# Cached keys of an encoder step copied in SBUF to an fp32r tile and transposed from it, for head pair 0 also transposed as fp32

## The chip, the cores and the metric

The kernel runs on one core of one Trainium2 chip. The metric is the device time of one execution in microseconds (us). The engines are named as in the profile: PE is TensorE (matmuls and transposes; PEld are its weight loads), DVE is VectorE, ACT is ScalarE, POOL is GpSimd, SP is SyncE, which here only issues DMAs. Each engine takes its own instructions in the order in which the kernel gives them. SBUF is the memory beside the engines (128 partitions), PSUM the one into which TensorE writes.

## The reference

One layer of a streaming encoder. 1024 new prompt frames and 64 frames of a running stream go through one input projection to 6144 columns; two attention branches with 8 heads of 64 follow, "sb" (stick breaking) and "cb" (a softmax over a band with a bias); their outputs are gated, projected, merged, projected again and added to the input. The change touches the keys of the running stream: its queries attend to 512 cached keys and the 64 new ones.

```python
# x_sample (1, 64, 1024); cache_sb_k, cache_cb_k (1, 1, 512, 8, 64)
sq2, sk2, sv2, sz2, cq2, ck2, cv2, cz2, gs2, gc2 = project(y_s, norm_w[l], w_in[l], q_norm_w[l], k_norm_w[l])
k_all = jnp.concatenate([cache_sb_k[l].astype(sk2.dtype), sk2], axis=1)
o_sb2 = stick_breaking(sq2, k_all, v_all, s_qpos, sb_s_kpos)
kb = jnp.concatenate([cache_cb_k[l].astype(ck2.dtype), ck2], axis=1)
o_cb2 = band_attention(cq2, kb, vb, s_qpos, cb_s_kpos, rel_bias[l])
```

Both attentions need the scores q.k, so the cached keys are needed with the head dimension in the partitions, that is transposed.

## The kernel before

All data is fp32. A matmul is made from operands of the type fp32r. A value that has to keep its precision is split: a high part, written as fp32r by ScalarE, and a low part, the difference, by VectorE or GpSimd. A product is then three matmuls (high by high, low by high, high by low).

The kernel's order is written out by hand; nothing is reordered by a scheduler. It has these stages, by the lines of their matmuls in the trace: a first projection whose result has the frames in the partitions (L464, 10.8 to 227.6 us), a second one with the columns in the partitions (L634, 227.7 to 405.5), attention with the rest of the projection filled in between (L773, L1024, L1115, 405.6 to 856.9), the projections of the two branches (L873, L917, to 926.0) and the last one (L1407, to 1013.6).

The change lies in the first stage. Its loop runs over `i`, eight groups of 256 columns (`NB`), and within it over `ti`, nine tiles of frames in the order `TO` = 8, 0, 1, ..., 7, where tile 8 holds the 64 frames of the running stream. One tile (i, ti) is:

- 24 matmuls (16 for tile 8) into a PSUM tile "acc" (L464); there are three such tiles, two in `psF` and one in `psA`, which serves every third tile;
- `post_nat` (L339), where one is due: two transposes of an older tile of queries or keys into the PSUM tile "pk" (L349), ScalarE's high part (L353), VectorE's low part (L354), and DMAs of whole blocks to DRAM;
- `evac_nat` (L296): for value columns (groups 0 and 5 for "sb", 6 and 7 for "cb") ScalarE copies to "vst", which has three buffers (L305), and SyncE stores it twice (L307, L309); for queries and keys of "cb" ScalarE copies and squares (L319, L320), VectorE sums (L321), GpSimd takes the power -1/2 (L248, L249). For tile 8 a fold of two halves comes before (`fold`, L292 and L293);
- `norm_nat` (L325) of the tile before: two multiplications by VectorE (L329, L330), and for keys a store (L334, L336);
- at set tiles, the splitting of the next group's weights (L115, L122) with the load of those after them (L109), and the steps on the cached keys.

The cached keys go through two steps. `cache_load` (L362) at (0, 4) for "sb" and at (2, 3) for "cb" loads the 512 x 512 keys of a branch into the SBUF tile "ck" (1 MB, one buffer; L365). `cache_pair` (L368) takes one pair of heads, that is 128 of the 512 columns, at (1, 1), (1, 4), (1, 7) and (2, 1) for "sb" and two groups later for "cb": four transposes into the PSUM tile "pc", which has one buffer in `psK` (L371), ScalarE's high part (L373), VectorE's low part (L374), and a store to DRAM (`rdma`, L51) from "hc". Attention loads that back much later. The tile "ck" is used once more, at (4, 2), for the bias table (L238).

`rdma` (L49) is a DMA on SyncE's queue with both sides taken as fp32. A transpose is a matmul whose weights are the tile to transpose, with the identity matrix `ident` streamed through.

Of the kernel before, what the change touches and what calls it, by code (L numbers as in the profile page):

```python
# [8 lines left out]
F32 = mybir.dt.float32  # L9
F32R = mybir.dt.float32r  # L10
AF = mybir.ActivationFunctionType
OP = mybir.AluOpType
# [20 lines left out]
def hybrid_step_kernel(ctx: ExitStack, tc: tile.TileContext, x_prompt, x_sample, c_sbk, c_sbv, c_cbk, c_cbv,  # L33
# [3 lines left out]
    V, A, G, TE, SP = nc.vector, nc.scalar, nc.gpsimd, nc.tensor, nc.sync  # L37
# [11 lines left out]
    def rdma(out, in_):  # L49
        out, in_ = (a if isinstance(a, bass.AP) else a[:] for a in (out, in_))  # L50
        SP.dma_start(out.bitcast(F32), in_.bitcast(F32))  # L51
# [42 lines left out]
    ident = consts.tile([128, 128], F32, name="ident")  # L94
# [103 lines left out]
    with ExitStack() as ph:  # L198
        sx = ExitStack()
        natx = sx.enter_context(tc.tile_pool(name="natx", bufs=2))  # L200
        pn = ph.enter_context(tc.tile_pool(name="pn", bufs=2, side="right"))
        p1x = ExitStack()
        p1 = p1x.enter_context(tc.tile_pool(name="p1", bufs=2))
        psA = ph.enter_context(tc.tile_pool(name="p1acc", bufs=1, space=PS))
        psT = ph.enter_context(tc.tile_pool(name="p1tr", bufs=2, space=PS))
        psK = ph.enter_context(tc.tile_pool(name="p1k", bufs=1, space=PS))
# [3 lines left out]
        xts, xns, hl, cks = {}, {}, {}, {}  # L210
# [19 lines left out]
        half = pn.tile([128, 8], F32, name="half", bufs=1)  # L230
        G.memset(half, -0.5)
        wqk = pn.tile([128, 2, 64], F32, name="wqk", bufs=1)

        rbs = {}

# [126 lines left out]
        def cache_load(b):  # L362
            src = c_sbk if b == "sb" else c_cbk
            ck = p1.tile([128, 4, 512], F32, name="ck", bufs=1)
            SP.dma_start(ck, src.rearrange("(t p) c -> p t c", p=128))  # L365
            cks[b] = ck

        def cache_pair(b, p):  # L368
            pt = psK.tile([128, 4, 128], F32, name="pc")
            for t in range(4):  # L370
                TE.transpose(pt[:, t], cks[b][:, t, p * 128:(p + 1) * 128], ident)  # L371
            h = p1.tile([128, 2, 512], F32R, name="hc", bufs=1)
            A.activation(h[:, 0], pt[:].rearrange("p t c -> p (t c)"), AF.Copy)  # L373
            V.tensor_tensor(out=h[:, 1], in0=pt[:].rearrange("p t c -> p (t c)"), in1=h[:, 0].bitcast(F32),  # L374
                            op=OP.subtract)
            rdma(d_cT[b][p], h)

        raws, blk, sums = {}, {}, {}
# [71 lines left out]
        for i in range(nb):  # L450
            for ti, t in enumerate(TO):
# [38 lines left out]
                if ti in (3, 6) and i > 0 or ti in (5, 6) and i == 0:  # L490
                    h = 1 if ti == 6 else 0
# [30 lines left out]
                if (i, ti) in ((0, 4), (2, 3)):  # L522
                    cache_load("sb" if i == 0 else "cb")
                at = {(1, 1): 0, (1, 4): 1, (1, 7): 2, (2, 1): 3}
                if (i, ti) in at:
                    cache_pair("sb", at[i, ti])
                if (i - 2, ti) in at:
                    cache_pair("cb", at[i - 2, ti])
                if (i, ti) in ((1, 1), (1, 5)):
                    for s in range(2):  # L530
                        h = ti // 4
# [637 lines left out]
    for i in range(len(seq) + LAG + 1):  # L1169
        m = 0  # L1170
        if i < len(seq):
            b, p, t, hd = seq[i]
# [22 lines left out]
        if 0 <= i - LAG < len(seq):  # L1195
            tr(i - LAG)
            b, p, t, hd = seq[i - LAG]
# [182 lines left out]
    for i in range(2):  # L1380
# [3 lines left out]
        for q, s in enumerate(OP_):  # L1384
# [14 lines left out]
            for c in range(2) if s != "b" else ():  # L1399
# [9 lines left out]
                p = ps[:]  # L1409
# [15 lines left out]
                if s in (3, 4, 5, 6):  # L1425
# [4 lines left out]
                    if s == 4:  # L1430
                        p, x = u3[c], xrs.pop((i, 1, 1, c))
# [61 lines left out]
```

## Time and profile before

| | us |
|---|---|
| three runs | 1012.43, 1017.04, 1018.64 |
| median | 1017.04 |
| profiled execution, its time | 1019.66 |
| profiled execution, its span (first to last instruction) | 1017.8 |
| first stage (L464), first to last matmul start | 10.8 to 227.6 |
| transposes of the cached keys (L371), 32 in all | 50.5 to 132.7 |

The mean granted TensorE clock of the profiled execution is 0.993 of full speed. In the rows of the profile that follow, a timeline row gives the start in us, the duration in us, engine, line, operation, output and inputs, and in brackets the idle time of that engine just before, with what ended it. A row of a stretch gives its length and the busy time of PE, PEld, DVE, ACT and POOL with their instruction counts, then the granted clock, the mean busy share of the DMA engines, and GB/s. A row of a group gives the count, the busy time in us and the mean ns of one. A row of DMA issues gives their number, the size of each and the median us from issue to landing.

### The profile page before, as it was taken

What the parts mean: (1) busy time and instruction counts of PE and PEld (TensorE: products, weight loads), DVE (VectorE), ACT (ScalarE), POOL (GpSimd) and SP (SyncE); (2) the same over time, 40 slices, a digit from 0 to 9 for tenths busy, and PEclk for the clock granted to TensorE, in tenths of its full rate; (3) what the DMA queues carried; (4) which work ended last, traced back from release to release, by engine and by line L of the source; (5) the groups of instructions that cost most, each with busy time, mean ns of one, the idle gap of its engine ahead of it and who ended that gap; (6) DMA issues with size and microseconds to landing.
All of it is one profiled execution on the core that took longest, in us unless ns stands there. A gap on an engine that the chain in (4) does not pass through costs nothing. (4 is left out here: it accounts for less than half of the span.)

```text
span 1017.8 us, 20166 instructions
## 1 busy us (share of the span) xinstructions
PE 983.5 (97%) x7512; PEld 935.4 (92%) x7512; DVE 658.2 (65%) x1233; ACT 474.2 (47%) x1075; POOL 323.9 (32%) x338
## 2 busy tenths in 40 slices
PE   6999999998999999999999999999999999899998
PEld 5999999998999999988888889898988898799998
DVE  5466663894455454199888877566766675588645
ACT  5544442343343433276667656444445443355220
POOL 3376663205354543211111101110103102375452
PEclk9999999999999999999999999999999999999999
DMA  7636467435556332786656554665667854852632
GB/s 239 213 114 206 174 244 278 126 94 155 178 159 178 102 96 84 198 213 181 163 153 164 144 146 126 175 205 150 175 159 213 248 174 148 257 159 70 192 124 97
DMA packets 180866, 169.83 MB, mean 167 GB/s; under 512 B 34913, under 2 KB 167137, under 8 KB 180641
## 3 DMA queue, kind: packets, MB, share of 16 engines
q1 hardware_dynamic: 172048, 160.23, 53.4%
q10 hardware_dynamic: 8720, 8.33, 2.6%
q8 instruction: 59, 0.97, 0.4%
q14 instruction: 39, 0.31, 0.1%
HBM read 109.78 MB, written 58.72 MB: 166 GB/s over the span
## 5 line engine op out<-in xcount | busy, mean ns | idle before, releaser
L122 POOL TENSOR_TENSOR wlo<-wraw,whi 128x1024 fp32r<-128x1024 f32 x30 | 73.8, 2459 | 247.5 <-ACT whi L115 227.0
L773 PE MATMUL acc<-xm,whi 128*128 128x384 f32 (+1 forms) x384 | 128.6, 335 | 0.0
L1044 DVE TENSOR_TENSOR_SCAN kp<-kp,imp 64x576 f32<-64x576 f32 (+8 forms) x72 | 102.7, 1427 | 21.4 <-ACT kp L1027 21.2
L1034 ACT ACTIVATE be<-be,sm 128x640 f32<-128x640 f32 (+5 forms) x72 | 50.8, 705 | 97.5 <-DVE sm L1030 97.5
L1076 PE MATMUL pt<-ident,be 128*128 128x128 f32 (+2 forms) x608 | 89.7, 271 | 6.3 <-DVE wT L1087 3.4
L1085 ACT ACTIVATE wT<-pt 128x512 f32<-128x512 f32 (+3 forms) x130 | 63.5, 502 | 54.9 <-PE pt L1076 54.7
L1076 PEld LDWEIGHTS pt<-ident,be 128*128 128x128 f32 (+2 forms) x608 | 68.2, 140 | 18.3 <-issue 6.4
L464 PE MATMUL acc<-whi,xa 128*128 128x256 f32 x256 | 74.2, 292 | 0.0
L773 PEld LDWEIGHTS acc<-xm,whi 128*128 128x128 f32 x384 | 72.5, 189 | 1.1
L464 PE MATMUL acc<-whi,xm 128*128 128x256 f32 x256 | 70.8, 278 | 0.0
L464 PE MATMUL acc<-wlox,xm 128*128 128x256 f32 x256 | 70.8, 278 | 0.0
L464 PE MATMUL acc<-wlo,xa 128*128 128x256 f32 x256 | 70.7, 278 | 0.0
L464 PE MATMUL acc<-whix,xb 128*128 128x256 f32 x256 | 70.7, 278 | 0.0
L464 PE MATMUL acc<-whix,xm 128*128 128x256 f32 x256 | 70.6, 278 | 0.0
L1115 PE MATMUL o<-wT,vp 128*64 128x256 f32 (+1 forms) x608 | 66.6, 360 | 0.0
L1045 DVE TENSOR_TENSOR be<-be,kp 64x576 f32<-64x576 f32 (+8 forms) x72 | 60.3, 837 | 9.6
L1027 ACT ACTIVATE kp<-z 128x384 f32<-128x384 f32 (+6 forms) x112 | 54.2, 484 | 24.4 <-PE z L1025 22.9
L773 PE MATMUL acc<-xa,wlo 128*128 128x384 f32 (+1 forms) x192 | 65.4, 341 | 0.0
L773 PE MATMUL acc<-xa,whi 128*128 128x384 f32 (+1 forms) x192 | 65.3, 340 | 0.0
L773 PE MATMUL acc<-xm,wlo 128*128 128x384 f32 (+1 forms) x192 | 65.1, 339 | 0.0
L1115 PEld LDWEIGHTS o<-wT,vp 128*64 128x64 f32 x608 | 42.7, 138 | 23.4 <-issue 8.0
L773 PE MATMUL acc<-xb,whi 128*128 128x384 f32 (+1 forms) x192 | 64.0, 334 | 0.0
(298 smaller groups left out, 3028.1 us busy)
## 6 DMA issues: line engine op xcount, KB each, us to landing
wraw<-in_w_in_dram SPq DMA_DIRECT2D x35, 512.0 KB, 4.5
wrawx<-in_w_in_dram SPq DMA_DIRECT2D x13, 512.0 KB, 4.3
sq<-d_qsbT SPq DMA_DIRECT2D x32, 192.0 KB, 4.4
sq<-d_qcbT SPq DMA_DIRECT2D x32, 192.0 KB, 4.0
gt<-d_gsb SPq DMA_DIRECT2D x30, 192.0 KB, 3.3
xt<-in_x_prompt_dram SPq DMA_DIRECT2D x8, 512.0 KB, 5.2
d_kcbT<-hl SPq DMA_DIRECT2D x8, 512.0 KB, 4.4
d_qcbT<-hl SPq DMA_DIRECT2D x8, 512.0 KB, 5.6
```

What stands on the lines that cost most here:

```text
L122: (eng or G).tensor_tensor(out=l, in0=raw, in1=h[:].bitcast(F32), op=OP.subtract)
L464: TE.matmul(ps, x, w, start=m == 0, stop=m == len(steps) - 1)
L773: TE.matmul(ps[:, :b - a], w[:, k], xk(x, k)[:, a:b], start=k == 0 and n == 0, stop=k == KT - 1 and n == 2)
L1027: A.activation(kp[:r, x:y], z[:r, :m], AF.Sigmoid, scale=-0.125)
L1034: A.activation(be[:r, :n], be[:r, :n], AF.Exp, bias=kp[:r, j:j + 1], scale=-1.0, accum_out=kp[:r, 2:3])
L1044: V.tensor_tensor_scan(kp[:r, n - 1::-1], kp[:r, n - 1::-1], im[:, ::-1], 0.0, op0=OP.mult, op1=OP.add)
L1045: V.tensor_tensor(out=be[:r, :n], in0=be[:r, :n], in1=kp[:r, 1:n + 1], op=OP.mult)
L1076: TE.transpose(pt[:kr, x, :r], be[:r, kb * 128:kb * 128 + kr], ident[:r, :r])
L1085: A.activation(w[:, sl:sl + m, q0:q0 + r], pt[:, :m, :r], AF.Copy)
L1115: TE.matmul(o[hd * 64:hd * 64 + 64, c0:c1], vv[:kr, kb, hd * 64:hd * 64 + 64], wT[b, p, j, hd, s // 4][:kr, s % 4, c0:c1], start=si == 0, ...
```

## The change

A second identity, `identr`, is made as fp32r. `cache_load` copies "ck" within SBUF, by a DMA, to a tile "cr" of type fp32r, and `cache_pair` transposes from that. For pair 0 of either branch the transposed tile is copied out of PSUM, the same keys are transposed from "ck" as fp32 into another tile of the name "pc", the difference of both is taken, multiplied by 8192 and added to the fp32 one, and this sum is split into high and low part.

```diff
         wqk = pn.tile([128, 2, 64], F32, name="wqk", bufs=1)
+        identr = pn.tile([128, 128], F32R, name="identr", bufs=1)
+        V.tensor_copy(identr, ident)
...
             SP.dma_start(ck, src.rearrange("(t p) c -> p t c", p=128))
-            cks[b] = ck
+            cr = p1.tile([128, 4, 512], F32R, name="cr", bufs=1)
+            rdma(cr, ck)
+            cks[b] = ck, cr
 
         def cache_pair(b, p):
-            pt = psK.tile([128, 4, 128], F32, name="pc")
+            pt = psK.tile([128, 4, 128], F32R, name="pc")
             for t in range(4):
-                TE.transpose(pt[:, t], cks[b][:, t, p * 128:(p + 1) * 128], ident)
+                TE.transpose(pt[:, t], cks[b][1][:, t, p * 128:(p + 1) * 128], identr)
+            src = pt[:].bitcast(F32).rearrange("p t c -> p (t c)")
+            if p == 0:
+
+                d = p1.tile([128, 512], F32, name="cd", bufs=1)
+                V.tensor_copy(d, src)
+                p2 = psK.tile([128, 4, 128], F32, name="pc")
+                for t in range(4):
+                    TE.transpose(p2[:, t], cks[b][0][:, t, p * 128:(p + 1) * 128], ident)
+                s2 = p2[:].rearrange("p t c -> p (t c)")
+                V.tensor_tensor(out=d, in0=s2, in1=d, op=OP.subtract)
+                V.scalar_tensor_tensor(d, d, 8192.0, s2, op0=OP.mult, op1=OP.add)
+                src = d[:]
             h = p1.tile([128, 2, 512], F32R, name="hc", bufs=1)
-            A.activation(h[:, 0], pt[:].rearrange("p t c -> p (t c)"), AF.Copy)
-            V.tensor_tensor(out=h[:, 1], in0=pt[:].rearrange("p t c -> p (t c)"), in1=h[:, 0].bitcast(F32),
-                            op=OP.subtract)
+            A.activation(h[:, 0], src, AF.Copy)
+            V.tensor_tensor(out=h[:, 1], in0=src, in1=h[:, 0].bitcast(F32), op=OP.subtract)
             rdma(d_cT[b][p], h)
```

## The prediction

> **What bounds the kernel now.** I read the busy shares first, then busy time by stretch, then the timelines of TensorE, VectorE, ScalarE and SyncE around the two places where the cached keys are loaded and transposed.
>
> ```profile
> span 1017.8 us, 20166 instructions
> ...
> PE 983.5 (97%) x7512; PEld 935.4 (92%) x7512; DVE 658.2 (65%) x1233; ACT 474.2 (47%) x1075; POOL 323.9 (32%) x338
> ```
>
> ```profile
> 50.00:60.00 10.00, 10.00 (x86) 9.80 (x85) 4.12 (x10) 3.55 (x9) 7.05 (x13) 1.00 0.36 114
> ...
> 104.00:112.00 8.00, 8.00 (x71) 8.00 (x71) 5.08 (x13) 2.98 (x10) 4.45 (x6) 1.00 0.51 182
> ```
>
> TensorE is busy for 97% of the span, and in the two stretches that hold pair 0 of "sb" and of "cb" it is never idle (10.00 of 10.00 us, 8.00 of 8.00). So whatever TensorE waits there is added to the end, and work on other engines or on the DMAs costs only what it makes TensorE wait. These are the instructions around pair 0 of either branch, on TensorE:
>
> ```profile
> 50.36 0.28 PE L464 MATMUL acc<-wlox,xm 128*128 128x256 f32 x1
> ...
> 50.48 0.60 PE L371 MATMUL pc<-ident,ck 128*128 128x128 f32 x4
> ...
> 50.84 0.36 PE L464 MATMUL acc<-whi,xa 128*128 128x256 f32 x1
> ...
> 51.04 0.28 PE L464 MATMUL acc<-whi,xm 128*128 128x256 f32 x1
> ...
> 104.75 0.60 PE L371 MATMUL pc<-ident,ck 128*128 128x128 f32 x4
> ...
> 105.10 0.36 PE L464 MATMUL acc<-whi,xa 128*128 128x256 f32 x1
> ```
>
> and on VectorE, with the nearest row for a copy of 128x512 out of PSUM behind them:
>
> ```profile
> 51.71 0.41 DVE L329 TENSOR_TENSOR qn<-qn,rsn 64x256 f32<-64x256 f32 x1
> ...
> 52.15 0.42 DVE L330 TENSOR_TENSOR qn<-qn,wqk 64x256 f32<-64x256 f32 x1
> 52.50 0.68 DVE L374 TENSOR_TENSOR hc<-pc,hc 128x512 fp32r<-128x512 f32 x1
> ...
> 106.69 0.42 DVE L330 TENSOR_TENSOR qn<-qn,wqk 64x256 f32<-64x256 f32 x1
> 107.04 0.68 DVE L374 TENSOR_TENSOR hc<-pc,hc 128x512 fp32r<-128x512 f32 x1
> ...
> L1087 DVE COPY wT<-pt 128x512 f32<-128x512 f32 x10 | 6.8, 683 | 1.7 <-PE pt L1076 1.7
> ```
>
> The reader is to see the distance between the two engines. TensorE has its four transposes away and is on the next tile at 50.84 and 105.10, while VectorE reaches its work on the same PSUM tile only at 52.50 and 107.04, since the normalisation of the tile before (L329, L330) stands ahead of it. Today nobody waits for that.
>
> **Pair 0: a new wait of TensorE, the main term.** The PSUM tile "pc" has one buffer. The new code transposes into it as fp32r, copies it out with VectorE, and transposes the same keys again, as fp32, into the same buffer. These second transposes wait for the copy, and all matmuls of the next tile are queued behind them on TensorE. The copy takes the place of L374 in VectorE's order: 52.50 + 0.68 = 53.18. From one engine's end to the next one's start I take 0.04 us, by the rows of the fold (47.85 + 0.38 to 48.27):
>
> ```profile
> 46.02 0.39 ACT L305 ACTIVATE vst<-acc 128x256 f32<-128x256 f32 x1 [2.44 <-PE acc L464]
> 47.85 0.38 ACT L292 ACTIVATE fl<-acc 64x256 f32<-64x256 f32 x1 [1.45 <-PE acc L464]
> ...
> 48.27 0.42 DVE L293 TENSOR_TENSOR fl<-acc,fl 64x256 f32<-64x256 f32 x1 [6.47 <-ACT fl L292]
> ...
> 50.25 1.01 POOL L249 TENSOR_TENSOR rsn<-rsn,half 64x4 f32<-64x4 f32 x1
> ```
>
> A group of four fp32 transposes costs 51.04 - 50.48 - 0.12 (the step from 50.36 to 50.48 is that of one matmul) = 0.44 us. So the next tile begins at 53.18 + 0.04 + 0.44 = 53.66 instead of 50.84: +2.8 us. For "cb": 107.04 + 0.68 + 0.04 + 0.44 = 108.20 instead of 105.10: +3.1 us. TensorE is idle 2.4 and 2.6 us of these.
>
> What follows on the pair (subtract 0.68, the scaled add 0.75 by L266's row below, ScalarE's copy, the low part) holds ScalarE's queue until about 3.1 us after the second transposes begin: 0.44 + 0.68 + 0.75 + 0.6 and VectorE's 0.68. ScalarE's next work is the eviction of the tile that TensorE has then just begun, 24 matmuls of 0.12 or 2.8 us behind the transposes' 0.44. It is free again before, so I cost this at nothing; the low part ends beside it. The copy of the identity at the start is one small VectorE instruction before VectorE's first input arrives: nothing.
>
> ```profile
> L266 DVE SCALAR_TENSOR_TENSOR xn<-xt,rs,nw 128x512 f32<-128x512 f32 x16 | 11.3, 747 | 5.7 <-POOL rs L249 5.6
> ...
> 579.45 0.22 PE L1024 MATMUL z<-ks,sq 128*128 128x128 f32 x1
> 579.51 0.28 PE L1025 MATMUL z<-ks,sq 128*128 128x128 f32 x1
> ```
>
> **The transposes in fp32r.** Pair 0's own are before the wait and cost nothing more. The other 24 (three pairs, two branches) go from fp32 at 0.11 to fp32r. No fp32r transpose is in the trace. Two fp32r matmuls of 128 columns stand 0.06 us apart (579.45, 579.51), one of 256 columns takes 0.12. So 24 transposes gain at most 24 x 0.05 = 1.2 us and lose at most 24 x 0.01 = 0.2. Between the row of the same operation and the row of the same type and size I take the middle: -0.6 us.
>
> **The copy in SBUF: two more DMAs of 1 MB, and a held queue.** The copy is issued by SyncE, in order, and waits there until "ck" has landed.
>
> ```profile
> 35.81 0.46 SPq L365 DMA_DIRECT2D ck<-in_cache_sb_k_dram  x1
> 37.64 0.32 SPq L307 DMA_DIRECT2D d_sbv<-vst  x1
> 38.01 0.64 SPq L309 DMA_DIRECT2D out_dram<-vst  x1
> ...
> 87.52 1.26 SPq L365 DMA_DIRECT2D ck<-in_cache_cb_k_dram  x1
> ...
> 95.99 0.36 SPq L336 DMA_DIRECT2D out_dram<-qn  x1
> ...
> ck<-in_cache_sb_k_dram SPq DMA_DIRECT2D x1, 1024.0 KB, 6.2
> ...
> ck<-in_cache_cb_k_dram SPq DMA_DIRECT2D x1, 1024.0 KB, 8.1
> ```
>
> For "sb", SyncE stands from 36.3 to 35.81 + 6.2 = 42.0. Then the copy goes out; no SBUF-to-SBUF transfer is in the trace, so by its own size in "ck"'s row it takes 6.2 (at the least some 5 us, at the most the 8.1 of the other load) and lands at 48.2. TensorE asks for it at 50.5, and even 1.6 us later would do, as VectorE is the last to come: the landing itself costs nothing. But the two stores of "vst" that stood at 37.64 and 38.01 now go out at 42.5 to 43.5, behind 1 MB, and land at about 48.9. "vst" has three buffers, so the eviction of the third tile after, at 46.02, waits for them: 48.9 instead. The fold behind it on ScalarE moves from 47.85 to 49.3, so by 1.4 us, and with it its chain (fold, squares, the power on GpSimd that ends at 51.26, L329). That chain had 0.45 us to spare (51.71 against 51.26), so L329, L330 and the copy move by 1.0 us, and TensorE's wait with them: +1.0 us. With a copy of 5 us it is 0, with one of 8.1 it is about 2.9. The weights whose load is held behind the stores are split two tiles and more later than they land.
>
> For "cb", SyncE had nothing to issue until 95.99, and "ck" lands at 95.6: the hold is nothing. The copy lands at 101.9 to 103.8, ahead of 104.75: nothing, with the landing before TensorE's request as cover.
>
> **The clock.** Idle time of this length has cost clock in this trace. Below are TensorE's three waits with one gap each, and the granted clock by microsecond (seventh figure).
>
> ```profile
> 253.52 0.44 PE L595 MATMUL acc<-ident,s 128*128 128x128 f32 x2 [3.00 <-ACT ko L601]
> ...
> 582.18 1.37 PE L1076 MATMUL pt<-ident,be 128*128 128x128 f32 x8 [2.40 <-DVE wT L1087]
> ...
> 946.69 2.66 PE L1407 MATMUL b<-wo,tk 128*128 128x256 f32 x16 [2.18 <-DVE fl L1449]
> ...
> 255.00:256.00 1.00, 1.00 (x11) 1.00 (x10) 0.51 (x2) 0.99 (x3) 0.00 (x0) 1.00 0.73 243
> ...
> 582.00:583.00 1.00, 0.82 (x7) 0.82 (x8) 1.00 (x2) 0.13 (x1) 0.00 (x0) 0.93 0.16 50
> ...
> 586.00:587.00 1.00, 1.00 (x12) 0.60 (x10) 0.00 (x0) 0.00 (x0) 0.00 (x0) 0.87 0.00 0
> ...
> 948.00:949.00 1.00, 1.00 (x8) 1.00 (x7) 0.22 (x1) 0.00 (x0) 0.00 (x0) 0.54 0.38 72
> ```
>
> Read as a clock of 1.00 or 0.50, these rows put the falls at 582.86 and 948.08 and the rise at 586.26. The stretch of 3.4 us fits a fixed grid, since 948.08 - 582.86 is 107 steps of 3.413 us. The gap of 2.40 us lies whole in the step that ends at 582.86, and the gap of 2.18 has 2.0 us in the step that ends at 948.08: both fell. The gap of 3.00 us is cut by the grid into 1.25 and 1.75 us, and the clock stayed. So a step with about 1.9 us of idle time or more halves the next 3.4 us of work, a price of 1.7 us less what of the gap runs on into it. How the grid lies against the start of another execution the trace can't tell. With the grid anywhere, a gap of 2.6 us ("cb") has 1.9 us in one step in (0.8 + 2 x 0.7) of 3.4 cases, 64%; the gap of "sb", 2.4 + 1.0 = 3.4 us, in 87%, with part of it running on. I take both as falling, at 1.3 and 1.6 us: +2.9 us.
>
> The Trainium skill, "TensorE: Matmul & The Clock Gate", under "Why this matters for your kernels", asks only for "No PE-idle gaps >~3µs between matmul bursts"; its Part 1 has a free-running window of 3413 ns. The window agrees with the grid above, the limit does not: 2.40 and 2.18 us sufficed here. By its limit the clock would stay, and the sum would lose the 2.9 us; that is the second rival.
>
> **The sum.** 2.8 + 3.1 (waits) + 1.0 (held queue) - 0.6 (transposes) + 2.9 (clock) = +9.2 us. The profiled execution took 1019.66 us, 1.86 more than its span, so it would become 1028.9. It is 2.6 above the median of the three runs, 1017.04; against that median I get **1026.2 us**.
>
> **The rivals.**
> Slower by over 1%: the copy in SBUF is slow. SBUF is read and written at once, which no row shows. From a landing at about 49.1 (7.1 us) the held stores cost 0.9 us more, which carries the sum over 1%; at 8.1 us it is 2.9 instead of 1.0: +11.1, 1028.1 us. For it speaks "ck" of "cb" at 8.1, against it that the queue is empty before the copy, having been held.
> The clock stays, or falls once: with one fall the sum is +7.8, with none +6.3, 1023.3 us. For it speaks the gap of 3.00 us that kept its clock, against it the two shorter ones.
> Not slower: the change doesn't do what it says to TensorE, since the second transposes get PSUM of their own beside the first and need not wait. Then there remain two groups of transposes, 0.9 us, less 0.6, and 1017.3 us. Against it: the tile has the same name and one buffer, and the kernel elsewhere takes "xm" anew under one name with another type.
>
> **How the numbers follow.** Forecast 0.45, slow copy 0.25, fewer clock falls 0.24, no wait 0.06. The low bound takes no held stores, the full gain of 1.2 and no fall: 2.8 + 3.1 - 1.2 = +4.7, 1021.7, less some spread of the runs shown (they differ by up to 6 us): 1020. The high bound takes 2.9 for the stores, no gain, both falls at 1.7: +12.2, 1029.2, and the same spread: 1032. The case without a wait and some of the tails stay out. A measurement of this kernel can tell about 1% from no change, 10.2 us here. Over it lie 0.4 of the forecast, three quarters of the slow copy and little of the rest, 0.39 together; faster is left 0.02, within 1% 0.59.
>
> **What would show it.** The timeline of TensorE should have a gap of 2.4 to 3.5 us before the second four transposes at about 51 and one of 2.6 at about 105 to 108, each ended by VectorE's copy; the next tile's matmuls straight after. SyncE should stand at the copy until about 42; ScalarE's eviction at 46.02 should move to about 49. The granted clock should fall to 0.5 for 3.4 us behind either gap. The forecast is wrong if the second transposes start before VectorE's copy ends, if the copy lands after 52, if TensorE waits at other places for evictions or for weights, or if later waits of TensorE shrink by what is lost here.

## The result, and the profile after

| | us |
|---|---|
| before, median of 18 runs (lowest to highest) | 1012.69 (1009.54 to 1018.74) |
| changed, median of 18 runs | 1019.85 (1016.25 to 1023.55) |
| ratio, 95% interval | 1.0058, 1.0041 to 1.0075 |
| profiled execution of the changed kernel, its time and its span | 1018.51, 1016.7 |

The changed kernel is slower by 0.58%, or 5.9 us (4.2 to 7.6) of the 1012.7 before; the two medians by themselves lie 7.2 us apart. The forecast was +9.2 us and 1026.2 us, its range began at 1020.0. The sign was right, the time lies 0.15 us under the range. Of the three runs of before from which the prediction had to start, two lie high among the 18 (1017.04 and 1018.64). Two of the twelve executions of one kernel further down, the changed kernel with its two waits filled, took 1248.78 and 1207.45 us at a granted clock of 0.730 and 0.755, and its median is that of the other ten.

TensorE's timeline of the changed kernel shows the new waits:

```profile
49.84 0.28 PE L479 MATMUL acc<-wlox,xm 128*128 128x256 f32 x1
49.96 0.45 PE L375 MATMUL pc<-identr,cr 128*128 128x128 f32 x4
52.83 0.66 PE L383 MATMUL pc<-ident,ck 128*128 128x128 f32 x4 [2.41 <-DVE cd L380]
53.24 0.36 PE L479 MATMUL acc<-whi,xa 128*128 128x256 f32 x1
53.44 0.28 PE L479 MATMUL acc<-whi,xm 128*128 128x256 f32 x1
...
106.87 0.53 PE L375 MATMUL pc<-identr,cr 128*128 128x128 f32 x4
109.97 0.43 PE L383 MATMUL pc<-ident,ck 128*128 128x128 f32 x1 [2.56 <-DVE cd L380]
```

and VectorE's the instructions that end them:

```profile
51.75 0.42 DVE L332 TENSOR_TENSOR qn<-qn,wqk 64x256 f32<-64x256 f32 x1
52.10 0.68 DVE L380 COPY cd<-pc 128x512 f32<-128x512 f32 x1
53.52 0.69 DVE L385 TENSOR_TENSOR cd<-pc,cd 128x512 f32<-128x512 f32 x1 [0.75 <-PE pc L383]
...
109.24 0.67 DVE L380 COPY cd<-pc 128x512 f32<-128x512 f32 x1
```

TensorE stands idle before the second transposes for 2.41 and 2.56 us, until the copy of the first is out of PSUM, and the copy begins behind L332, where L374 began before. In TensorE's list of waits over the whole span (engine, line, what it waited for: us in total, times, longest) this is the one new group:

```profile
PE pc L383 <- DVE cd L380: 5.0, 2, 2.6
```

5.0 us of waits and 2 x 0.44 us of transposes make 5.9. This execution is nevertheless 1.1 us shorter in its span than the profiled one of before (1016.7 to 1017.8). The reason is elsewhere: that one had waited 3.1 + 1.6 us for weights at 885 us (L917), with a fall of the clock of 6.8 us behind it, and this one 1.1 us. One execution each says nothing about a change of 6 us here; the medians do.

On SyncE and ScalarE the held queue is seen (the last row is one of DMA issues, with the median us to landing):

```profile
35.29 0.46 SPq L367 DMA_DIRECT2D ck<-in_cache_sb_k_dram  x1
41.92 0.50 SPq L51 DMA_DIRECT2D cr<-ck  x1
42.52 0.53 SPq L309 DMA_DIRECT2D d_sbv<-vst  x1
43.11 1.12 SPq L311 DMA_DIRECT2D out_dram<-vst  x1
...
47.46 0.39 ACT L307 ACTIVATE vst<-acc 128x256 f32<-128x256 f32 x1 [4.40 <-DMA out_dram<-vst]
47.87 0.38 ACT L294 ACTIVATE fl<-acc 64x256 f32<-64x256 f32 x1
...
cr<-ck SPq DMA_DIRECT2D x2, 1024.0 KB, 4.9
```

SyncE stands until 41.92, the stores go out behind the copy, and ScalarE waits for them 4.40 us. It is done at 47.85, and the fold begins at 47.87. This execution is 0.5 us ahead of the other there (35.29 against 35.81 for the load), so the fold is 0.5 us late, as much as the chain behind it had to spare: VectorE's copy at 52.10 is 0.1 us later than 52.50 - 0.52. The hold is there and costs next to nothing.

The granted clock (seventh figure) behind the two waits:

```profile
53.00:54.00 1.00, 1.00 (x10) 1.00 (x10) 0.48 (x1) 0.00 (x0) 1.00 (x5) 1.00 0.43 105
...
110.00:111.00 1.00, 1.00 (x5) 1.00 (x6) 0.00 (x0) 0.00 (x0) 0.19 (x1) 0.53 0.00 0
...
113.00:114.00 1.00, 1.00 (x8) 1.00 (x8) 0.69 (x1) 0.15 (x1) 0.00 (x0) 0.77 0.00 0
```

It fell behind the second, from 110.06 to 113.46, and not behind the first.

### The profile page after: what moved, and what is told of

The parts are those of the page before. It is cut to its first block, busy times and chain, and to the rows that moved or that the text cites. A ratio compares the mean times of both kernels' runs of the same rounds, so it can differ in the third digit from the quotient of the medians.

```text
span 1016.7 us, 20197 instructions
## 1 busy us (share of the span) xinstructions
PE 982.3 (97%) x7520; PEld 933.3 (92%) x7520; DVE 660.4 (65%) x1240; ACT 474.5 (47%) x1075; POOL 323.2 (32%) x338
```

## The experiments

The kernels of one set ran on one chip beside the kernel before; the ratios are to that.

### The changed kernel again, as the yardstick

> The changed kernel once more, as the yardstick of the runs beside it. Theory W (TensorE waits for the copy of pair 0 in the one PSUM tile, 2.4 and 2.6 us, pays 0.44 us for each of the two added groups of transposes, and now and then loses 1.7 us to a fall of the clock after a wait): 5.9 us and up to some 2 us more than before. Rival D (the copy in SBUF and its held queue carry a part) and rival T (the fp32r transposes give something back) expect the same of this run.

Measured: 1019.82 us against 1014.63, ratio 1.0057 (1.0037 to 1.0076). The same as in the first set.

### A PSUM tile of its own for the second transposes

```diff
-                p2 = psK.tile([128, 4, 128], F32, name="pc")
+                p2 = psK.tile([128, 4, 128], F32, name="pc2")
```

> The fp32 transposes of pair 0 go to a PSUM tile of their own, so TensorE need not wait for VectorE's copy. W: both gaps vanish, what is left is 0.9 us for the two added groups of transposes, so 0 to 2 us above before and 5 to 7 us under the changed kernel. D: the gaps vanish, but 2 us or more stay. T: at or under before.

Measured: 1014.20 us, ratio 0.9983 (0.9968 to 0.9998). The timeline of TensorE, and of VectorE below it:

```profile
50.17 0.46 PE L375 MATMUL pc<-identr,cr 128*128 128x128 f32 x4
50.47 0.62 PE L383 MATMUL pc<-ident,ck 128*128 128x128 f32 x4
50.85 0.36 PE L479 MATMUL acc<-whi,xa 128*128 128x256 f32 x1
...
52.22 0.68 DVE L380 COPY cd<-pc 128x512 f32<-128x512 f32 x1
```

The eight transposes go through back to back and the next tile starts at 50.85, while VectorE comes to its copy at 52.22, as late as ever. All of VectorE's added work is still there, and the whole loss is gone. So the loss is TensorE's wait for the one PSUM tile. By W 0.9 us should have stayed; the interval ends at 0.2 us under before. About 0.4 us of this the fp32r transposes of the other pairs give back, as the next experiment shows; the rest is not explained.

### The copy in SBUF and the fp32r transposes alone

```diff
-            if p == 0:
+            if p < 0:
```

> The copy in SBUF and the fp32r transposes of all pairs stay, the second transposes of pair 0 with their copy, difference, product and sum are left out. W: within 1 us of before, though ScalarE's eviction is held to about 47.5 us for the stores behind the copy. D: 2 us or more above before. T: 0.5 to 1 us under before, beyond what can be told from this run alone; the timeline then has four fp32r transposes in less than the 0.44 us of the fp32 ones.

Measured: 1011.66 us, ratio 0.9979 (0.9959 to 0.9999). ScalarE's timeline shows the same hold as in the changed kernel:

```profile
47.18 0.39 ACT L307 ACTIVATE vst<-acc 128x256 f32<-128x256 f32 x1 [3.78 <-DMA out_dram<-vst]
47.59 0.38 ACT L294 ACTIVATE fl<-acc 64x256 f32<-64x256 f32 x1
```

Two more DMAs of 1 MB and a queue that stands 6 us cost nothing that shows; rival D falls. That it came out 2 us under before is more than any of the three expected, and is taken up below.

For the fp32r transposes the timeline of a later pair decides. Pair 3 of "sb", in the kernel before and in the changed one, with two transposes of another tile (`pk`) in front of it:

```profile
77.50 0.38 PE L349 MATMUL pk<-ident,qn 128*128 128x128 f32 x2
77.72 0.60 PE L371 MATMUL pc<-ident,ck 128*128 128x128 f32 x4
...
78.27 0.28 PE L464 MATMUL acc<-whi,xm 128*128 128x256 f32 x1
```

```profile
79.86 0.38 PE L351 MATMUL pk<-ident,qn 128*128 128x128 f32 x2
79.99 0.53 PE L375 MATMUL pc<-identr,cr 128*128 128x128 f32 x4
...
80.55 0.28 PE L479 MATMUL acc<-whi,xm 128*128 128x256 f32 x1
```

From the start of the two transposes in front to the same matmul behind the four, it is 78.27 - 77.50 = 0.77 us before and 80.55 - 79.86 = 0.69 us after. The time has to be taken from the same instruction in front: the fp32r group itself starts earlier behind it (0.13 us against 0.22), so from its own start it seems to take as long as the fp32 one, 0.44 us. By this measure every group gains 0.06 to 0.08 us, which makes some 0.4 us for the six groups of pairs 1 to 3. So rival T is right that the fp32r transposes give something back, but it is too little to be told from the times.

### Pair 0 twice as fp32, without the copy

```diff
-            cr = p1.tile([128, 4, 512], F32R, name="cr", bufs=1)
-            rdma(cr, ck)
-            cks[b] = ck, cr
+            cks[b] = ck, ck
...
-            pt = psK.tile([128, 4, 128], F32R, name="pc")
+            pt = psK.tile([128, 4, 128], F32, name="pc")
...
-                TE.transpose(pt[:, t], cks[b][1][:, t, p * 128:(p + 1) * 128], identr)
+                TE.transpose(pt[:, t], cks[b][1][:, t, p * 128:(p + 1) * 128], ident)
```

> No copy in SBUF and no fp32r: the keys of pair 0 are transposed twice as fp32 from the loaded tile, with the copy, difference, product and sum. W: as the changed kernel, 5 to 8 us above before, with the same two gaps of TensorE. D: clearly less than the changed kernel, by 2 us or more. T: above the changed kernel by up to 1 us.

Measured: 1021.72 us, ratio 1.0057 (1.0032 to 1.0081). TensorE has the two waits without the copy too, a little shorter:

```profile
52.71 0.66 PE L381 MATMUL pc<-ident,ck 128*128 128x128 f32 x4 [2.14 <-DVE cd L378]
...
111.57 1.12 PE L381 MATMUL pc<-ident,ck 128*128 128x128 f32 x4 [2.42 <-DVE cd L378]
```

This part alone carries the change.

### All pairs, and the waits filled with matmuls

What is open is the clock. Treating all pairs like pair 0 makes eight waits of two:

```diff
-            if p == 0:
+            if True:
```

> All four pairs of both branches are treated as pair 0 is, so six more waits of TensorE. By the changed kernel's trace VectorE would begin the copy for these at 65.0, 74.9, 82.5, 122.9, 132.5 and 140.0 us, which makes idle times of about 2.6 to 3.6 us, 18.6 together, and 0.44 us for each added group of transposes, 2.6. Theory C (a wait of this length also makes the clock fall behind it in most cases, at up to 1.7 us): 21 us for the waits and transposes and some 5 to 9 us for the clock above the changed kernel, 26 to 30 us in all. Rival N (the clock plays no part that can be seen): 21 us, plus or minus 2.

Measured over five executions: 1048.54 us against 1013.53, ratio 1.0341 (1.0309 to 1.0373), 28.7 us above the changed kernel's 1019.85: C, not N. In a second kernel TensorE is kept busy in the waits, whose end is set by VectorE as before:

```diff
+                dm = psK.tile([128, 256], F32, name="dm")
+                for t in range(18):
+                    TE.matmul(dm, xs[:, t % KT], W.sp[gi[0], 0][0][:, t % 4], start=t == 0, stop=t == 17)
                 p2 = psK.tile([128, 4, 128], F32, name="pc")
```

> As the kernel with all pairs, and in each of the eight waits TensorE does 18 matmuls of 128x256 into a PSUM tile of their own that nobody reads (2.1 us), so the waits last as long but are hardly idle. C: no falls of the clock there, 6 to 11 us under the kernel with all pairs. N: the same as that kernel, or above it where a wait is shorter than its filling.

Measured over four executions: 1038.62 us, ratio 1.0234 (1.0200 to 1.0268). The mean granted clock of its runs is 0.995, that of the kernel without the filling 0.984. In TensorE's timeline the second transposes start when they did, only most of the idle time before them is gone (52.86 here, 52.87 without the filling; from the first transposes to the second ones all eight waits last 23.5 us here and 23.2 us there, of which TensorE is idle 6.3 and 23.2):

```profile
50.28 2.28 PE L385 MATMUL dm<-whi,xs 128*128 128x256 f32 x18
52.86 0.65 PE L388 MATMUL pc<-ident,ck 128*128 128x128 f32 x4 [0.30 <-DVE cd L382]
```

1048.54 - 1038.62 = 9.9 us for eight waits: an idle wait of 2.3 to 3.5 us costs 1.2 us more than the same wait with work in most of it.

The rule by which the prediction read the falls can be tried on the eight waits, whose rows are these:

```profile
52.87 0.66 PE L383 MATMUL pc<-ident,ck 128*128 128x128 f32 x4 [2.28 <-DVE cd L380]
67.23 0.66 PE L383 MATMUL pc<-ident,ck 128*128 128x128 f32 x4 [2.97 <-DVE cd L380]
82.22 1.12 PE L383 MATMUL pc<-ident,ck 128*128 128x128 f32 x4 [3.54 <-DVE cd L380]
96.68 0.66 PE L383 MATMUL pc<-ident,ck 128*128 128x128 f32 x4 [2.56 <-DVE cd L380]
126.78 0.66 PE L383 MATMUL pc<-ident,ck 128*128 128x128 f32 x4 [2.57 <-DVE cd L380]
140.35 1.11 PE L383 MATMUL pc<-ident,ck 128*128 128x128 f32 x4 [3.24 <-DVE cd L380]
156.49 1.08 PE L383 MATMUL pc<-ident,ck 128*128 128x128 f32 x4 [3.52 <-DVE cd L380]
169.74 0.70 PE L383 MATMUL pc<-ident,ck 128*128 128x128 f32 x4 [2.56 <-DVE cd L380]
```

and the clock by microsecond at the falls:

```profile
54.00:55.00 1.00, 1.00 (x8) 1.00 (x7) 0.95 (x2) 0.00 (x0) 0.05 (x1) 0.58 0.02 8
67.00:68.00 1.00, 0.77 (x6) 0.77 (x7) 0.25 (x2) 0.00 (x0) 0.44 (x1) 0.91 0.00 0
81.00:82.00 1.00, 0.00 (x0) 0.00 (x0) 0.96 (x3) 0.00 (x0) 0.92 (x2) 0.74 0.09 12
139.00:140.00 1.00, 0.00 (x0) 0.00 (x0) 0.96 (x3) 0.00 (x0) 0.88 (x2) 0.75 1.07 377
156.00:157.00 1.00, 0.51 (x3) 0.51 (x4) 0.44 (x1) 0.00 (x0) 0.70 (x1) 0.78 0.53 163
170.00:171.00 1.00, 1.00 (x8) 1.00 (x7) 0.52 (x1) 0.00 (x0) 0.00 (x0) 0.61 0.00 0
```

The first fall is at 55 - 2 x 0.42 = 54.16, the others likewise at 67.82, 81.48, 139.50, 156.56 and 170.22. All lie on steps of 3.413 us from 54.16. Cutting the waits with that grid:

| wait | idle, us | most of it in one step, us | clock |
|---|---|---|---|
| 50.59 to 52.87 | 2.28 | 2.12 | fell at 54.16 |
| 64.26 to 67.23 | 2.97 | 2.83 | fell at 67.82 |
| 78.68 to 82.22 | 3.54 | 2.80 | fell at 81.48 |
| 94.12 to 96.68 | 2.56 | 1.55 | stayed |
| 124.21 to 126.78 | 2.57 | 1.64 | stayed |
| 137.11 to 140.35 | 3.24 | 2.39 | fell at 139.50 |
| 152.97 to 156.49 | 3.52 | 3.34 | fell at 156.56 |
| 167.18 to 169.74 | 2.56 | 2.56 | fell at 170.22 |

Eight of eight follow the rule, and three waits of 2.56 to 2.57 us went both ways by where the grid cut them. The two waits of the changed kernel agree: with the fall at 110.06 the first is cut into 1.61 and 0.80 us and kept its clock, the second lies whole in one step and lost it.

### The changed kernel with its two waits filled

The same 18 matmuls, in the waits of pair 0 alone.

> The changed kernel with the same 18 matmuls in its two waits. C: 1 to 3 us under the changed kernel; the granted clock stays at 1.00 behind both waits. N: the same as the changed kernel.

Measured: 1015.99 us, ratio 1.0018 (0.9995 to 1.0041), against 1.0057 for the changed kernel: 3.9 us less by the medians. The direction is C's, the size is above its 1 to 3 us. The clock of the ten executions averages 0.997, against 0.9945 over 30 runs of the changed kernel, worth 2.4 us; the rest is not explained. Seen from the kernel before, the filled waits and the added transposes should still cost some 5.5 us, and 1.8 (-0.5 to 4.2) is measured; the clock, 0.997 against 0.9955, accounts for 1.4 us of the difference, and 2.3 us stay open. No profile of this kernel at a clock near 1.00 is on record, so it is not shown that the clock stays at 1.00 behind both waits, nor how long the waits were.

### The copy twice

The held queue was worth 1.0 us in the prediction and nothing in the result. Whether that is so because the mechanism is absent, or because it stays within a margin, is told by a longer hold:

```diff
             rdma(cr, ck)
+            rdma(cr, ck)
```

> The copy in SBUF is done twice, one behind the other, so SyncE stands some 4.6 us longer (the copy's own time in the changed kernel). Theory H (the held stores cost nothing as long as ScalarE's eviction starts before the fold would, at 47.9 us, and pass on each us beyond that to VectorE's copy): the stores land at about 52, the fold begins at 52.4, TensorE's first wait grows by about 4.5 us, and the kernel takes 4 to 6 us more than the changed one. Rival F (a held queue costs nothing here at all): the same as the changed kernel.

Measured: 1027.06 us, ratio 1.0125 (1.0094 to 1.0155), 7.2 us above the changed kernel. SyncE, ScalarE, VectorE and TensorE in turn, and a row of TensorE's list of waits:

```profile
41.73 5.05 SPq L51 DMA_DIRECT2D cr<-ck  x2
...
47.47 1.10 SPq L311 DMA_DIRECT2D out_dram<-vst  x1
...
51.80 0.39 ACT L307 ACTIVATE vst<-acc 128x256 f32<-128x256 f32 x1 [8.49 <-DMA out_dram<-vst]
52.21 0.38 ACT L294 ACTIVATE fl<-acc 64x256 f32<-64x256 f32 x1
...
56.44 0.68 DVE L381 COPY cd<-pc 128x512 f32<-128x512 f32 x1
...
57.17 1.11 PE L384 MATMUL pc<-ident,ck 128*128 128x128 f32 x4 [5.76 <-DVE cd L381]
...
PE pc L376 <- DMA cr<-ck: 1.7, 2, 1.2
```

The chain is the one that was expected, with the fold at 52.21 (52.4 was expected) and TensorE's wait at 5.76 us, with 0.5 us more in front of the first transposes. H holds in its mechanism, F falls; the 7.2 us are above H's 4 to 6. "cb" lost 1.2 us as well (the longest in the last row), since the second copy landed after TensorE asked for it, which H did not foresee. TensorE's first wait grew by 3.4 us and that of "cb" by 0.3, so with the 0.5 and the 1.2 us in front of the first transposes this makes some 5.3 us. The rest, 1.9 us, fits the clock: it averages 0.991 against 0.9945, worth 3.8 us, but in the profile it is at half speed from 53.21 to 60.04, and TensorE is waiting until 57.17 of that, where a low clock costs nothing.

### Is there a gain in the copy?

The two kernels without waits were 1.7 and 2.1 us under before. Four more runs bear on that: the kernel before as if it were a change, the kernel with the copy alone again, the kernel before with an unused tile in the copy's place, and pair 0 without the copy again.

```diff
+            if b == "sb":
+                p1.tile([128, 4, 512], F32R, name="cr", bufs=1)
             cks[b] = ck
```

> The kernel before, run as if it were a change, to see what these comparisons give where nothing differs: within 2 us of before. What is open: the kernels with the copy and without TensorE's waits came out 1.7 and 2.1 us under before, at the edge of their intervals. Theory Z: that is scatter. Rival S: the copy, or the 10 KB more that its tiles take in SBUF, makes something later 2 us faster.

> The kernel with the copy and the fp32r transposes alone, once more. The second transposes of pair 0 with their copy, difference, product and sum are left out. Z: within 1.5 us of before. S: 2 us under it again.

> The kernel before with nothing but an unused tile of 8 KB per partition in the place of the copy's, so that all tiles behind it lie elsewhere in SBUF. Z: within 1.5 us of before. S, if it is the place in SBUF: 2 us under before; if it is the copy itself: as before.

> Pair 0 transposed twice as fp32, no copy in SBUF, once more, since the first had only seven runs. Z: as the changed kernel, 5 to 7 us above before. S: some 2 us above the changed kernel, 7 to 9 above before.

Measured, against 1014.45 us:

| kernel | median, us | ratio, 95% interval |
|---|---|---|
| the kernel before itself | 1014.22 | 1.0009, 0.9989 to 1.0029 |
| copy alone | 1012.75 | 0.9988, 0.9967 to 1.0009 |
| unused tile alone | 1011.79 | 0.9986, 0.9965 to 1.0007 |
| pair 0 without the copy | 1020.93 | 1.0069, 1.0042 to 1.0096 |

All that was to be told apart lies within the intervals. The kernel with the copy alone lies under before again, the kernel with the unused tile and no copy does too, and pair 0 without the copy is again no lower than the changed kernel. That would fit a gain of 1 to 2 us from where tiles lie in SBUF, but a kernel against itself moves by 0.9 us by the ratio. It stays open. That the copy costs no more than about 1 us is shown; that it gains is not. Of the 2 us of the kernel with the copy, the fp32r transposes explain about a quarter.

## Why the prediction was wrong, point by point

The mechanism was right; what failed were sizes. The base was taken as 1017.04 us and measured as 1012.69, the term for the clock was +2.9 us and measured as 1.0, and the term for the held queue was +1.0 us and measured as nothing.

- **The wait of TensorE for the copy of pair 0 (+2.8 and +3.1 us): right.** Foreseen were idle times of 2.4 and 2.6 us and 0.44 us for each group of transposes; the profile has 2.41 and 2.56, and for the group 53.44 - 52.83 - 0.12 = 0.49 by the prediction's own measure. The PSUM tile of its own takes the loss away, pair 0 alone brings all of it.
- **What follows on the pair on VectorE and ScalarE (nothing): right.** ScalarE is through with the pair's copy before the next tile is to be evicted, and in the kernel with two tiles all this work is there at no loss.
- **The held queue (+1.0 us): the term was mis-sized, its chain was right.** The step took 6.2 us for the copy, by the row of the load of the same size. It took 4.6 (and 5.2 for "cb"), so the stores landed by 47.46, not 48.9, inside the margin of 1.85 us that the step itself gave (1.4 on ScalarE, 0.45 behind GpSimd). The copy done twice shows the chain paying once the margin is used up. The bound of "some 5 us" with a cost of 0, for which the prediction gave no row, was the right end. For "cb" the copy was foreseen as free, and was.
- **The fp32r transposes (-0.6 us): near, it is some -0.4.** The 24 transposes gained 0.06 to 0.08 us per group of four, or 0.015 to 0.02 each. The forecast was the middle between two rows and no mechanism, so that it came this close is luck.
- **The clock (+2.9 us): the mechanism was right, the size was not.** Where the grid falls isn't known beforehand; both waits were taken as losing the clock, as the likeliest single case. In the changed kernel's first profile one of two did, and over 30 runs of it the mean granted clock is 0.9945, against 0.9955 over 76 of the kernel before. That is 0.0010 of 1017 us, or 1.0 us, with a standard error of 0.5 us by the scatter of the runs. The wait of "sb" being 2.4 us and not 3.4, its chance was nearer to (1.0 + 2 x 0.5) of 3.4, 59%, than 87%; with 64% for "cb" the mean is 1.2 falls, 2.1 us, and the measured 1.0 us is less still. In the four profiles that have just these two waits (two of the changed kernel, two of pair 0 without the copy) four of the eight waits lost the clock, so one fall per execution. The mean would have been the better figure here, since each run draws anew and a median of many runs lies near it.
- **The base.** The sum was laid on the median of three runs, 1017.04. Over 76 runs of the kernel before in later sets it is 1014.5, and 1012.7 in the set of the result. The spread that the clock makes from run to run (4 of the 30 runs of the changed kernel at a clock of 0.998 took 1016.25 to 1018.65 us, 6 at 0.991 and 0.992 took 1021.15 to 1024.29) means that three runs place a median only to some 2 to 4 us. The low end took 1.7 us for this.
- **The sum.** 5.9 (waits and transposes) + 0 (held queue) - 0.4 (fp32r) + 1.0 (clock) = 6.5 us, against 5.9 (4.2 to 7.6) measured. The time fell out of the range, by 0.15 us, through the base, 4.4 us lower than taken, and the terms for the clock and the queue, 2.9 us too large together. The base alone would have sufficed: laid on 1012.69, the same sum gives 1021.9 us and the same range 1015.6 to 1027.7, and 1019.85 lies inside.
- **The rivals.** The slow copy didn't come: it took 4.6 to 5.2 us, not 7.1 or more. The case without a wait is the kernel with two PSUM tiles, and that gives the time of the kernel before. The case of fewer falls (+6.3 to +7.8) came nearest, and the page of the Trainium skill, "TensorE: Matmul & The Clock Gate", is still not borne out by its limit of about 3 us: waits of 2.28 and 2.56 us lost the clock.

## What to carry to other kernels

An operation that reuses a PSUM tile which has one buffer waits for the last reader of that tile, and that reader starts where its engine's queue lets it, not when the data is ready. Here 0.7 us of copying made 2.4 us of waiting, and a second PSUM tile took it away. When a queue is held, look for the first buffer that runs out behind it and count its margin: up to that margin the hold is free, beyond it every microsecond is paid.

Where idle time of TensorE of some 2 us or more can't be avoided, matmuls whose result nobody reads were cheaper than idling here (9.9 us over eight waits). And a forecast of half a per cent needs a base from more than three runs.

## What the runs showed of the hardware

- The granted clock is decided on a fixed grid of 3.413 us whose place differs from run to run. In the waits followed above, 1.83 us of idle time or less within one step kept the clock and 2.02 us or more halved it for the next step. The 1.83 is the wait of "cb" in the second profile of the changed kernel, 107.50 to 110.07, cut at 109.33; the 2.02 was in the kernel before at 945. Worked out in the same way for every step at full speed, from the first rise of the clock on, in the profiles of all kernels here but the changed one with its waits filled, each of the 42 steps with 1.92 us or more was followed by half speed and each with 1.80 us or less by full speed. Between these it went either way: 1.83 us in the step from 782.38 in a later profile of the kernel before (the run against itself) lost the clock, 1.89 us in the step from 256.10 in the second profile of the changed kernel kept it. A step at half speed with 0.75 us and one with 0.85 us of idle time in it were followed by another (81.48 and 139.50 in the table's kernel, two steps each); those with 0.54 us or less were followed by full speed.
- A copy of 1 MB within SBUF took 4.6 to 5.2 us from issue to landing in the changed kernel and 4.5 to 5.6 us over all profiles here, the load of the same size from DRAM 5.7 to 8.5 us.
- Four transposes of 128x128 took 0.06 to 0.08 us less as fp32r than as fp32, where a fp32 one takes 0.11 us.
